# Two vector-matrix products of a diffusion step, moved from TensorE strips to VectorE sums

## The chip, the cores and the metric

The kernel runs on one core of a Trainium2 chip. The metric is device time in microseconds (us) of one execution. The kernel before takes 1458.52 us (median of 3 runs, 1456.28 to 1462.25).

## The reference: what is computed

One layer of a hybrid backbone works on 128 context tokens and 512 latent tokens of width 2048, in float32. Cut to what matters here:

```python
silu_c, silu_ctx = silu(c), silu(c_ctx)[None]
mod_ctx = silu_ctx @ w_mod[i] + b_mod[i]            # (1, 6144): shift, scale, gate
mod_lat = silu_c @ w_mod[i] + b_mod[i]
h = _rms_norm(x, norm_w) * (1.0 + scale[:, None]) + shift[:, None]
proj = h @ w_in                                     # 2048 -> 7216: u_f, z_f, q, k, v, z_d, a, b
y_f = _fourier_mix(u_f, grid) * silu(z_f)           # 4 groups of 128 columns
o_fw, s_fw = _chunk_gated_delta(q, k, v, ...)       # 12 heads of 128, forward and backward
y_d = _rms_norm(o, gnorm_w) * silu(z_d)
y = concatenate([y_f, y_d]) @ w_out
x + gate[:, None] * y                               # then a final RMS norm
```

Two pieces of it are products of a vector with a matrix, each for two vectors (latent and context): the gate third of `mod`, which is `silu(c) @ w_mod[:, 4096:6144]` and the same with `c_ctx`, and the shift's share of the Fourier inputs, `shift @ w_in[:, 0:512]`. The second exists because the kernel multiplies `x * scale` without the shift, and adds the shift's product as a bias of each column afterwards.

## The kernel before, in words

**The stream.** The input projection runs on TensorE as 53 column tiles of 128 columns ("u" Fourier inputs, "f" their gates, "k", "v", "q", "z" of the heads). Float32 is split into a high and a low part, so a tile takes three products for each of 16 blocks of 128 rows, for each of two halves of 320 tokens: 96 products, all at line 1354 (`stream`). The weights are cast to the high part by ScalarE (line 1330) and subtracted to the low part by GpSimd (line 1338).

**The heads.** A head's q, k and v go through convolution, the blocks of its triangular matrix, their inversion (`solve`, lines 872 to 945), `decay` (lines 950 to 1000), `prep` (1005 to 1050) and the scan (1058 to 1143). These are small products on TensorE (lines 929, 940, 973, 994, 1012, 1025, 1040, 1047, 1072, 1079, 1091, 1099, 1111) with VectorE, ScalarE and GpSimd work and small transfers through memory between them. `solve` writes its blocks to memory and reads them back as tiles DD and DP by eight transfers (lines 912 and 915); VectorE transposes DD (line 918) and TensorE multiplies with it (line 929). The k and q tiles of head h may only be evacuated when head h-2 has been scanned.

**What sets the order.** Each step is a Python generator. While the program is written, a planner (`Estimate`, lines 55 to 210) keeps an estimated clock for every engine. It writes stream products, and between any two steps of six products it lets every generator go on whose inputs are due by that estimate; smaller ranks go first. So the order on every engine is fixed when the program is built, and each engine runs its own queue in order. `yield "V", t` means "go on when VectorE is free and estimated time t has come", `"P"` the same for TensorE, `"S"` for the queue SP that issues transfers.

**The two vector products before.** `rows256` (line 1264) works on 256 columns at a time. It loads four blocks of 128 rows by one transfer of 512 KB into the tile gw (line 1269), and multiplies: four products, each with one column strip of 32 of TensorE's array, whose stationary operand is the two vectors padded with zeros to 32 columns (line 1273). VectorE adds the four results to ga (lines 1276 and 1278). After four such loads one product with `sel_mod` (a matrix of zeros and ones) adds the four strips (lines 1260 and 1291). `shift_u` calls it twice, `res_gates` eight times, so line 1273 holds 40 groups of four products. They have the largest rank, 10, of all steps. The tile gw is one buffer. A product of two float32 operands stands as two instructions in the profile.

**Names.** csh and cz are the two vectors (shift, silu of c), of 16 x 32 columns, of which the first two of each 32 hold them. gates_d is the gates' row in memory, which the output stage reads back. L1622 is the output product.

## Time and profile before

| | us |
|---|---|
| median of 3 runs | 1458.52 |
| lowest, highest | 1456.28, 1462.25 |
| the profiled execution's own time | 1462.74 |
| its span, first to last instruction | 1460.9 |
| TensorE busy in the span | 1400.6 |
| VectorE busy | 695.1 |
| ScalarE busy | 670.8 |
| GpSimd busy | 627.6 |

The span is the time from the first to the last instruction on the core; 1.8 us of the execution lie outside it. PE is TensorE, DVE VectorE, ACT ScalarE, POOL GpSimd, SP the queue that issues transfers. A product's row gives its start and how long it stays in the array; since products are pipelined, the step from one start to the next is what a product costs in a row of them.

### The profile page before, as it was taken

The page shows a single profiled execution, that of the slowest core. Times are in us where ns is not written, and L with a number is a line of the kernel's source. Part 1 is how long each engine was busy: PE and PEld are TensorE (multiplying, and loading weights), DVE is VectorE, ACT ScalarE, POOL GpSimd, SP SyncE. Part 2 cuts the span into 40 slices and gives each one's busy share as a digit, 9 for nine tenths or more (in the row PEclk, how much of TensorE's full clock was granted, in tenths as well). Part 3 has the DMA queues.
Part 4 walks back from the last instruction along what each step waited for, and adds up shares of the span by engine and source line. Part 5 has one row for each costly group of instructions (what it writes and reads, how often), then busy time and mean ns, then how long its engine had stood idle before and what let it go on. Part 6 is the DMA issues. An engine that isn't in the chain of part 4 may idle for free.

```text
span 1460.9 us, 31546 instructions
## 1 busy us (share of the span) xinstructions
PE 1400.6 (96%) x12548; PEld 1272.2 (87%) x12548; DVE 695.1 (48%) x1476; ACT 670.8 (46%) x1808; POOL 627.6 (43%) x649
## 2 busy tenths in 40 slices
PE   6999989999999999999999999999999998999996
PEld 4799869878999889889999999899999996888885
DVE  5441115664346644746474646457463745322025
ACT  5332226634456445354555555455555454323134
POOL 2233213443334534344464544545364442337375
PEclk9999989999999999999999999999999999999998
DMA  9988973553454533433233333333242435494103
GB/s 304 271 264 267 309 202 105 151 147 102 140 146 123 141 124 95 144 106 90 83 91 87 86 107 83 106 87 106 72 112 62 137 111 178 148 323 163 44 1 144
DMA packets 268880, 203.21 MB, mean 139 GB/s; under 512 B 54649, under 2 KB 238918, under 8 KB 268606
## 3 DMA queue, kind: packets, MB, share of 16 engines
q1 hardware_dynamic: 146110, 129.36, 28.9%
q10 hardware_dynamic: 122624, 71.84, 17.1%
q8 instruction: 99, 1.62, 0.5%
q14 instruction: 47, 0.39, 0.1%
HBM read 177.16 MB, written 23.99 MB: 138 GB/s over the span
## 4 chain that ended last, share of the span: by engine, by line
PE 75%; DVE 9%; DMA 6%; ACT 2%; SPq 2%; issue 2%; POOL 1%; DVEq 0%; ACTq 0%; POOLq 0%
PE mbank L1354 40%; PE bank L1622 8%; PE mbank L1622 7%; PE bank L430 2%; DVE tmp L898 2%; PE bank L1091 1%; DMA DD<-xd 1%; PE bank L1111 1%; PE bank L1099 1%; PE bank L1072 1%; DVE tmp L885 1%; PE bank L1079 1%; PE bank L1273 1%; PE bank L587 1%; SPq L875 1%
## 5 line engine op out<-in xcount | busy, mean ns | idle before, releaser
L1338 POOL TENSOR_TENSOR wlo<-raw,whi 128x512 fp32r<-128x512 f32 x232 | 327.0, 1413 | 550.4 <-ACT whi L1330 463.0
L1354 PE MATMUL mbank<-h_hi,whi 128*128 128x320 f32 (+1 forms) x1696 | 556.0, 328 | 0.0
L1354 PE MATMUL mbank<-h_lo,whi 128*128 128x320 f32 (+1 forms) x1696 | 528.0, 311 | 0.0
L1354 PE MATMUL mbank<-h_hi,wlo 128*128 128x320 f32 (+1 forms) x1696 | 527.9, 311 | 0.0
L1354 PEld LDWEIGHTS mbank<-h_hi,whi 128*128 128x128 f32 x1696 | 321.9, 190 | 24.7 <-issue 20.3
L1354 PEld LDWEIGHTS mbank<-h_lo,whi 128*128 128x128 f32 x1696 | 322.3, 190 | 0.1
L1354 PEld LDWEIGHTS mbank<-h_hi,wlo 128*128 128x128 f32 x1696 | 321.9, 190 | 0.0
L1330 ACT CAST whi<-raw 128x512 fp32r<-128x512 f32 x232 | 142.2, 619 | 226.1 <-PE mbank L1354 155.3
L283 POOL TENSOR_TENSOR wlo<-raw,whi 128x512 fp32r<-128x512 f32 (+1 forms) x44 | 55.2, 1264 | 87.0 <-ACT whi L282 72.8
L1622 PE MATMUL mbank<-wlo,y_hi 128*128 128x512 f32 x160 | 63.7, 398 | 2.6 <-POOL wlo L283 2.0
L1622 PE MATMUL mbank<-whi,y_lo 128*128 128x512 f32 x160 | 64.1, 401 | 2.1 <-DVE y_lo L1509 2.0
L1622 PE MATMUL mbank<-whi,y_hi 128*128 128x512 f32 x160 | 64.1, 401 | 1.3 <-ACT y_hi L1507 1.3
L1094 ACT ACTIVATE vn<-bank,s 128x128 f32<-128x128 f32 x120 | 37.4, 364 | 57.1 <-PE bank L1091 56.7
L1622 PE MATMUL bank<-whi,y_hi 128*128 128x512 f32 x160 | 63.2, 395 | 0.0
L1622 PE MATMUL bank<-wlo,y_hi 128*128 128x512 f32 x160 | 63.1, 395 | 0.0
L1622 PE MATMUL bank<-whi,y_lo 128*128 128x512 f32 x160 | 63.1, 395 | 0.0
L1106 DVE SCALAR_TENSOR_TENSOR S<-S,egl,bank 128x128 f32<-128x128 f32 x72 | 21.8, 344 | 77.7 <-PE bank L1099 77.6
L282 ACT CAST whi<-raw 128x512 fp32r<-128x512 f32 (+1 forms) x44 | 24.6, 578 | 57.0 <-PE bank L1622 18.6
L885 DVE TENSOR_TENSOR tmp<-NP,XB 40x4 f32<-40x4 f32 (+6 forms) x84 | 31.1, 371 | 33.3 <-DMA NP<-pd 26.6
L1084 POOL TENSOR_SCALAR kd<-k,edl 128x128 f32<-128x128 f32 x96 | 45.4, 487 | 0.3
L977 ACT ACTIVATE E<-gb,ngg 128x128 f32<-128x128 f32 x120 | 40.2, 397 | 11.6 <-DVE AT L980 9.3
L829 POOL TENSOR_TENSOR nk<-sk,cst 128x5 f32<-128x5 f32 x12 | 14.1, 1179 | 63.2 <-DVE sk L826 56.3
(336 smaller groups left out, 2452.7 us busy)
## 6 DMA issues: line engine op xcount, KB each, us to landing
raw<-in_w_in ACTq DMA_DIRECT2D x106, 512.0 KB
wm<-in_w_mod SPq DMA_DIRECT2D x64, 512.0 KB
gw<-in_w_mod SPq DMA_DIRECT2D x32, 512.0 KB
raw<-in_w_out ACTq DMA_DIRECT2D x48, 256.0 KB
gb<-gd SPq DMA_DIRECT2D x12, 640.0 KB
yd<-zs SPq DMA_DIRECT2D x16, 320.0 KB
yt<-yd SPq DMA_DIRECT2D x16, 320.0 KB
out<-res SPq DMA_DIRECT2D x10, 512.0 KB
```

The lines of the kernel that those rows point to most:

```text
L282: ACT.copy(whi, raw_part)
L283: sub.tensor_tensor(wlo, raw_part, whi, ALU.subtract)
L430: PE.matmul(acc_a[i][:, 0:384], lhsT=w, rhs=h[kt][:, 256:NT], start=kt + n == 0, stop=last)
L885: DVE.tensor_tensor(tv, NPd[:, :, i, 0:i].unsqueeze(2).broadcast_to(s4), Xd[:, :, 0:i, 0:i].rearrange("p h j c -> p h c j"), ALU.mult)
L898: DVE.tensor_tensor(tv, A.unsqueeze(2).broadcast_to(s4), B.rearrange("p j c -> p c j").unsqueeze(1).broadcast_to(s4), ALU.mult)
L977: ACT.activation(E[:, 1 - d], gb[:, d, P * t:P * (t + 1)], AF.Exp, bias=ngg4[:, d, h, t:t + 1])
L1084: POOL.tensor_scalar(kd[:, d], k[:, tt[d], :], edl4[:, d, h, tt[d]:tt[d] + 1], 1.0, ALU.mult, ALU.mult)
L1094: ACT.mul(vn[:, d], pv[:, P * d:P * (d + 1)], s["s3"][:, d, tt[d]:tt[d] + 1])
L1330: ACT.copy(his[c], raws[c // 2][:, 4 * (c % 2):4 * (c % 2) + 4])
L1338: POOL.tensor_tensor(lo, raws[c // 2][:, 4 * (c % 2):4 * (c % 2) + 4], his[c], ALU.subtract)
L1354: PE.matmul(pm[:, 0:b - a], lhsT=w, rhs=h[k][:, a:b], start=k + m == 0, stop=k == NK - 1 and m == 2)
L1622: PE.matmul(acc[t], lhsT=a[kk][:, sl], rhs=w, start=kk == order[0] and j == 0, stop=kk == order[-1] and j == 2)
```

## The change

`rows256` no longer multiplies on TensorE. It loads two blocks of 128 rows (256 KB) at a time into the first half of the tile gw, and VectorE multiplies each block with one column of csh or cz, a value for each partition, and adds it to a sum for each of the two vectors in the other half of the tile. So the 2048 rows are summed to 128 partitions. The partitions are then summed by a product with ones: in `shift_u` four products of one column instead of two of two columns, in `res_gates` four strips of 32 columns, each for 128 of the columns of one vector, instead of one product with `sel_mod`. The bias b_mod is loaded, and the gates stored, by four transfers each instead of one.

Two planner rules are changed: a transfer now keeps the issuing queue for 0.4 us of the estimate instead of 0.06, and `solve` goes on to its transpose of DD only when 1.5 us have passed since the estimated landing. The Fourier gate tile f2, which stood between f1 and k2, stands after z10, in front of f3.

```diff
         if by == "DMA":
-            self.free[engine] = t + 0.06
+            self.free[engine] = t + 0.4
...
-        yield "V"
+        yield "V", est.written(DD) + 1.5
         f2, N = "p d t c -> p (d t c)", s["N"]
         DVE.transpose(DD[:, 2:4].rearrange(f2), DD[:, 0:2].rearrange(f2))
...
+    def rows256(src, by):
+        x = g.tile([P, 4, 256], F32, tag="gw", name="gw", bufs=1)
+        gw, acc = x[:, 0:2], x[:, 2:4]
+        for j in range(NK // 2):
+            SP.dma_start(out=gw, in_=src[:, 2 * j:2 * j + 2])
+            yield "V", est.last + 1.0
+            for q in range(2):
+                for m in range(2):
+                    one = by[:, 2 * j + q, m:m + 1]
+                    if j + q:
+                        DVE.scalar_tensor_tensor(acc[:, m], gw[:, q], one, acc[:, m], ALU.mult, ALU.add)
+                    else:
+                        DVE.tensor_scalar(acc[:, m], gw[:, q], one, None, ALU.mult)
+        yield
+        return x
...
-            ga = yield from rows256(win_v[:, :, 256 * i:256 * i + 256], csh)
+            x = yield from rows256(win_v[:, :, 256 * i:256 * i + 256], csh)
             pg = bank()
             for q in range(2):
-                PE.matmul(pg[:, 2 * q:2 * q + 2], lhsT=ga[:, P * q:P * (q + 1)], rhs=K("sel_mod"), start=True, stop=True)
+                for m in range(2):
+                    PE.matmul(pg[:, 2 * q + m:2 * q + m + 1], lhsT=x[:, 2 + m, P * q:P * (q + 1)], rhs=K("ones")[:, 0:1],
+                              start=True, stop=True)
...
-        for j in range(4):
-            gw = g.tile([P, 4, 256], F32, tag="gw", name="gw", bufs=1)
-            SP.dma_start(out=gw, in_=src[:, 4 * j:4 * j + 4])
-            yield "P", est.last + 3.0
-            pg = bank()
-            for q in range(4):
-                PE.matmul(pg[32 * q:32 * q + 32, 0:256], lhsT=lhs[:, 4 * j + q, :], rhs=gw[:, q, :], start=True, stop=True,
-                          tile_position=(0, 32 * q))
...
+            for b in range(4):
+                SP.dma_start(out=bt[32 * b:32 * b + 32], in_=b_mod[0, n0 + P * (b % 2):n0 + P * (b % 2) + P].partition_broadcast(32))
             yield "P", est.last + 1.0
             pg = bank()
-            PE.matmul(pg[0:2, 0:256], lhsT=K("sel_mod"), rhs=ga, start=True, stop=True)
-            DVE.tensor_tensor(bt, bt, pg[0:2, 0:256], ALU.add)
+            for b in range(4):
+                PE.matmul(pg[32 * b:32 * b + 32, 0:P], lhsT=K("ones")[:, 0:32], rhs=x[:, 2 + b // 2, P * (b % 2):P * (b % 2) + P],
+                          start=True, stop=True, tile_position=(0, 32 * b))
+            DVE.tensor_tensor(bt, bt, pg[:, 0:P], ALU.add)
...
-    names = "u0 u1 u2 u3 k1 q1 v1 z0 z1 f0 f1 f2".split()
-    fill = {2: "", 11: "z10 f3 z11"}
+    names = "u0 u1 u2 u3 k1 q1 v1 z0 z1 f0 f1".split()
+    fill = {2: "", 11: "z10 f2 f3 z11"}
```

Since the planner writes the order, rows move on every engine. Lines behind 1310 stand six lines lower in the changed file (L1354 is L1360 there, L1622 is L1628).

The first place is TensorE's queue in the scan of head 0. L1099 and L1111 end a scan step, L1072 and L1079 begin the next with the state S, L1091 uses r, which VectorE makes at line 1075. Before:

```order
L1099 MATMUL bank<-vn,kd 128x128 x2
L1111 MATMUL bank<-vn,AT 128x128 x2
L1354 MATMUL mbank<-h_hi,whi 128x320
L1354 MATMUL mbank<-h_lo,whi 128x320
L1354 MATMUL mbank<-h_hi,wlo 128x320
...
L1072 MATMUL bank<-S,KT 128x128 x2
L1079 MATMUL bank<-S,QT 128x128 x2
L1273 MATMUL bank<-gw,cz 32x256 x4
L1091 MATMUL bank<-r,KK 128x128 x2
```

And with the change:

```order
L1099 MATMUL bank<-vn,kd 128x128 x2
L1111 MATMUL bank<-vn,AT 128x128 x2
L1072 MATMUL bank<-S,KT 128x128 x2
L1079 MATMUL bank<-S,QT 128x128 x2
L1360 MATMUL mbank<-h_hi,whi 128x320
L1360 MATMUL mbank<-h_lo,whi 128x320
L1360 MATMUL mbank<-h_hi,wlo 128x320
...
L1091 MATMUL bank<-r,KK 128x128 x2
```

The four strips of line 1273 are gone, and stream products stand between line 1079 and line 1091 where they stood.

The second place is VectorE's queue at the start of the scan of head 1 (the row of L1125 is its first). Before:

```order
L1125 TENSOR_TENSOR o<-o,bank 128x128
L1075 SCALAR_TENSOR_TENSOR r<-bank,neg_eg,v 128x128 x2
L795 SCALAR_TENSOR_TENSOR zs<-zs,pj_1297 128x128
L795 SCALAR_TENSOR_TENSOR zs<-zs,pj_1297 128x512
L1276 TENSOR_TENSOR ga<-ga,bank 128x256
L1106 SCALAR_TENSOR_TENSOR S<-S,egl,bank 128x128 x2
L1121 TENSOR_TENSOR o<-o,bank 128x128 x2
```

With the change:

```order
L1125 TENSOR_TENSOR o<-o,bank 128x128
L1075 SCALAR_TENSOR_TENSOR r<-bank,neg_eg,v 128x128 x2
L1264 SCALAR_TENSOR_TENSOR gw<-gw,cz 128x256 x4
L826 TENSOR_SCALAR sk<-sk 128x5
...
L1106 SCALAR_TENSOR_TENSOR S<-S,egl,bank 128x128 x2
L1121 TENSOR_TENSOR o<-o,bank 128x128 x2
L1264 SCALAR_TENSOR_TENSOR gw<-gw,cz 128x256 x4
L1075 SCALAR_TENSOR_TENSOR r<-bank,neg_eg,v 128x128 x2
```

Batches of four multiply-adds of the loaded rows stand ahead of S (line 1106) and of r (line 1075), on which the next products of the scan wait. There are 80 such batches in all, the last ahead of the stream's 4260th product of 5088; the last use of line 1273 stood behind its 2442nd.

The third place is the end of the stream on TensorE, where head 11 is scanned. Before, the last scan products stand in a row, behind the stream's last product and ahead of the first output product (L1622):

```order
L1354 MATMUL mbank<-h_hi,wlo 128x322
L1099 MATMUL bank<-vn,kd 128x128 x2
L1111 MATMUL bank<-vn,AT 128x128 x2
L1072 MATMUL bank<-S,KT 128x128 x2
L1079 MATMUL bank<-S,QT 128x128 x2
L1091 MATMUL bank<-r,KK 128x128 x2
L1111 MATMUL bank<-vn,AT 128x128 x2
L1214 MATMUL bank<-dft,uT 128x256
```

With the change:

```order
L1099 MATMUL bank<-vn,kd 128x128 x2
L1111 MATMUL bank<-vn,AT 128x128 x2
L1360 MATMUL mbank<-h_hi,whi 128x322
...
L1072 MATMUL bank<-S,KT 128x128 x2
L1079 MATMUL bank<-S,QT 128x128 x2
L1360 MATMUL mbank<-h_hi,whi 128x322
...
L1091 MATMUL bank<-r,KK 128x128 x2
L1214 MATMUL bank<-dft,fx 128x256 x2
L1360 MATMUL mbank<-h_hi,whi 128x322
...
L1111 MATMUL bank<-vn,AT 128x128 x2
```

Six stream products stand between each of the last steps of the scan now, and 96 more behind its last product.

More of the change, by code (lines that the diff above doesn't have):

```diff
@@ L1263, in shift_u @@
         done.add("ubias")
-    def rows256(src, lhs):
-        ga = g.tile([P, 256], F32, tag="ga", name="ga", bufs=1)
-        for j in range(4):
-            gw = g.tile([P, 4, 256], F32, tag="gw", name="gw", bufs=1)
-            SP.dma_start(out=gw, in_=src[:, 4 * j:4 * j + 4])
-            yield "P", est.last + 3.0
-            pg = bank()
-            for q in range(4):
-                PE.matmul(pg[32 * q:32 * q + 32, 0:256], lhsT=lhs[:, 4 * j + q, :], rhs=gw[:, q, :], start=True, stop=True,
-                          tile_position=(0, 32 * q))
-            if j:
-                DVE.tensor_tensor(ga, ga, pg[:, 0:256], ALU.add)
-            else:
-                DVE.tensor_copy(ga, pg[:, 0:256])
-        yield
-        return ga
     def res_gates():
@@ L1284, in res_gates @@
         for i in range(8):
-            ns = slice(2 * DM + 256 * i, 2 * DM + 256 * i + 256)
-            ga = yield from rows256(wmv[:, :, ns], cz)
-            bt = g.tile([P, 4, 256], F32, tag="gw", name="gbt", bufs=1)[0:2, 0]
-            SP.dma_start(out=bt, in_=b_mod[0, ns].partition_broadcast(2))
+            n0 = 2 * DM + 256 * i
+            x = yield from rows256(wmv[:, :, n0:n0 + 256], cz)
+            bt = x[:, 0, 0:P]
+            for b in range(4):
+                SP.dma_start(out=bt[32 * b:32 * b + 32], in_=b_mod[0, n0 + P * (b % 2):n0 + P * (b % 2) + P].partition_broadcast(32))
             yield "P", est.last + 1.0
             pg = bank()
-            PE.matmul(pg[0:2, 0:256], lhsT=K("sel_mod"), rhs=ga, start=True, stop=True)
-            DVE.tensor_tensor(bt, bt, pg[0:2, 0:256], ALU.add)
+            for b in range(4):
+                PE.matmul(pg[32 * b:32 * b + 32, 0:P], lhsT=K("ones")[:, 0:32], rhs=x[:, 2 + b // 2, P * (b % 2):P * (b % 2) + P],
+                          start=True, stop=True, tile_position=(0, 32 * b))
+            DVE.tensor_tensor(bt, bt, pg[:, 0:P], ALU.add)
             yield "S"
-            SP.dma_start(out=gates_d[:, 256 * i:256 * i + 256], in_=bt)
+            for b in range(4):
+                SP.dma_start(out=gates_d[b // 2:b // 2 + 1, 256 * i + P * (b % 2):256 * i + P * (b % 2) + P], in_=bt[32 * b:32 * b + 1])
             yield
```

## The prediction

> **What bounds the kernel now.** I read the page first, then TensorE's time line around one of the removed groups, then busy time by stretch, then who waited for whom.
>
> ```profile
> span 1460.9 us, 31546 instructions
> PE 1400.6 (96%) x12548; PEld 1272.2 (87%) x12548; DVE 695.1 (48%) x1476; ACT 670.8 (46%) x1808; POOL 627.6 (43%) x649
> ...
> PE 75%; DVE 9%; DMA 6%; ACT 2%; SPq 2%; issue 2%; POOL 1%; DVEq 0%; ACTq 0%; POOLq 0%
> ...
> L1354 PE MATMUL mbank<-h_hi,wlo 128*128 128x320 f32 (+1 forms) x1696 | 527.9, 311 | 0.0
> ```
>
> TensorE is busy for 96% of the span, and the stream (line 1354) never stood idle for its inputs (last column 0.0). The chain that ended last runs over TensorE for 75% and over others for a quarter: TensorE is the bound, but the heads' small steps are close behind it. By stretch (window, length, then busy us of each engine, the granted clock behind POOL):
>
> ```profile
> 205.00:663.00 458.00, 440.40 (x4396) 400.55 (x4397) 241.18 (x529) 228.05 (x639) 184.81 (x205) 0.97 0.44 127
> 663.00:1075.00 412.00, 408.49 (x4171) 398.42 (x4170) 239.68 (x500) 219.57 (x633) 203.19 (x211) 1.00 0.33 90
> 205.00:1075.00 870.00, 848.90 (x8564) 798.97 (x8565) 480.86 (x1028) 447.63 (x1272) 388.00 (x415) 0.99 0.39 109
> ```
>
> The 40 groups of line 1273 run in the first of these; TensorE is idle there for 17.6 us of 458, and for 3.5 of the next 412. A product taken off TensorE here should therefore come off the span, unless a wait takes its place.
>
> **What the change removes from TensorE.** One group of four strips, alone in the stream (start, length, then what it is):
>
> ```profile
> 293.03 0.31 PE L1354 MATMUL mbank<-h_lo,whi 128*128 128x320 f32 x1
> 293.18 0.31 PE L1354 MATMUL mbank<-h_hi,wlo 128*128 128x320 f32 x1
> 293.42 0.64 PE L1273 MATMUL bank<-gw,cz 128*32 128x256 f32 x8
> 293.99 0.41 PE L1354 MATMUL mbank<-h_hi,whi 128*128 128x320 f32 x1
> ```
>
> Stream products start 0.15 us apart. Around the group two starts are 0.81 apart, so the group costs 0.66 us. Forty of them: 26.4 us. The busy time of the two groups of rows of this line agrees (20.4 and 5.9 us):
>
> ```profile
> L1273 PE MATMUL bank<-gw,cz 128*32 128x256 f32 x256 | 20.4, 390 | 0.0
> L1273 PE MATMUL bank<-gw,csh 128*32 128x256 f32 x64 | 5.9, 448 | 0.9 <-DMA gw<-in_w_in 0.9
> ```
>
> The sums over strips, in the same view of time (start to next start):
>
> ```profile
> 331.95 0.59 PE L1291 MATMUL bank<-ga,cst 128*2 128x256 f32 x2
> 332.47 0.41 PE L1354 MATMUL mbank<-h_hi,whi 128*128 128x322 f32 x1
> ...
> 298.33 0.48 PE L994 MATMUL bank<-jq,cst 128*32 128x160 f32 x8
> 298.74 0.41 PE L1354 MATMUL mbank<-h_hi,whi 128*128 128x320 f32 x1
> ...
> 240.04 0.50 PE L1260 MATMUL bank<-cst,ga 128*128 128x2 f32 x4
> 240.41 0.39 PE L1354 MATMUL mbank<-h_hi,whi 128*128 128x320 f32 x1
> ```
>
> Line 1291 costs 0.52 us, eight times 4.2. In its place stand four strips with ones; line 994 is the same product with 160 columns instead of 128 and costs 0.41, so at most 3.3 for eight. Line 1260 is two products for 0.37; four products of one column instead cost at most twice that, so the two calls go from 0.7 to 1.5. TensorE's net work: -26.4 - 4.2 + 3.3 - 0.7 + 1.5 = **-26.5 us**. The tile f2 costs the same where it stands now.
>
> **What else moves.** TensorE's waits from 205 to 1215 us, from the waits by engine (who waited for what, total us, times, longest):
>
> ```profile
> PE bank L929 <- DVE DD L918: 8.9, 9, 3.3
> PE bank L1260 <- DVE ga L1276: 1.0, 1, 1.0
> PE bank L1273 <- DMA gw<-in_w_in: 0.9, 2, 0.6
> PE bank L1111 <- ACT vn L1094: 0.8, 1, 0.8
> PE bank L1091 <- DVE r L1075: 0.6, 1, 0.6
> PE bank L1291 <- ACT KK L844: 0.3, 1, 0.3
> ```
>
> The waits of lines 1273, 1260 and 1291 (2.2 us) go with their products, or come back once as VectorE's. Those of lines 1111 and 1091 (1.4 us) are the two last steps of head 11's scan, which had no stream product between them. Now f2 lies there: **-1.4**. The f2 tile's 96 products (96 x 0.15 = 14 us) are missing between f1 and k2, but nothing there waits: k2's evacuation needs head 0's scan, whose last product stands 54 stream products ahead of it.
>
> L929 waits for the transpose of DD, and that for the eight transfers of DD and DP, which SP issues one after the other:
>
> ```profile
> 288.13 0.31 SPq L912 DMA_DIRECT2D DD<-xd  x1
> 288.50 0.45 SPq L915 DMA_DIRECT2D DP<-xd  x1
> ```
>
> One issue takes 0.31 to 0.45 us; the planner had reckoned 0.06, so it believed DD there some 8 x 0.35 = 3 us too early. With 0.4 and the margin of 1.5 us the transpose and its product are written later, and the wait can be filled with stream products. Between 0 and all of it: 0 to -8.9; one long wait there also cost clock:
>
> ```profile
> 606.00:609.70 3.70, 1.24 (x83) 1.20 (x84) 0.51 (x1) 0.37 (x3) 0.52 (x1) 1.00 0.45 123
> 609.70:613.10 3.40, 3.40 (x13) 2.23 (x11) 0.41 (x1) 0.70 (x3) 0.00 (x0) 0.50 0.34 104
> ```
>
> After 2.5 us of idleness the clock is granted at 0.50 for 3.4 us, which is another 1.7. I take half the 8.9, **-4.5**, as the other half may be a wait of which the queue's issue is not the cause.
>
> **What it adds on VectorE.** 300 multiply-adds and 20 multiplications of 128x256; the 40 additions and copies of ga go. No multiply-add of this size from SBUF is in the trace. The nearest is line 979, the same size with both inputs in SBUF (minimum, median, maximum ns, then the mean); with it, GpSimd's subtraction of the stream's low parts, and the additions that go:
>
> ```profile
> L979 DVE TENSOR_TENSOR KK<-KK,E x60: 380/412/1521, 265.3 to 1160.2; 128x256 f32<-128x256 f32 x60
> L979 DVE TENSOR_TENSOR KK<-KK,E 128x256 f32<-128x256 f32 x60 | 33.4, 557 | 1.5 <-ACT E L977 1.4
> L1338 POOL TENSOR_TENSOR wlo<-raw,whi x232: 1262/1289/2266, 96.0 to 1278.0; 128x512 fp32r<-128x512 f32 x116
> L1276 DVE TENSOR_TENSOR ga<-ga,bank 128x256 f32<-128x256 f32 x30 | 12.4, 414 | 24.3 <-PE bank L1273 24.1
> ```
>
> Between 412 and 557 ns each; I take the mean, since GpSimd works through the same stretch as beside line 979: 320 x 0.557 = 178 us, less 40 x 0.414 = 17 for the ga operations, so 161. VectorE was busy for 481 of the 870 us over which the batches now lie: 55% becomes 74%. The work itself is covered. If it were not, the uncovered part would come on top of the span one for one.
>
> The Trainium skill ("SBUF — State Buffer", section "Who interferes with whom") says that a VectorE instruction with two SBUF inputs contends with a GpSimd instruction that reads SBUF, and that whichever is second is fully blocked. Line 979's maximum, 1.1 us above its median, is as long as most of one subtraction, so the trace agrees; by that rule all 300 multiply-adds are such instructions. It is the reason for the second case below, whose sum stands on the rows above.
>
> What does not hide is lateness: VectorE's queue is in order, and r and S of the scan stand behind batches. A batch is late by its load and by GpSimd. The load: line 1273 waited 0.9 us in two waits, 0.45 each, with a margin of 3.0 us; with 1.0 I allow 0 to 0.45 per batch, up to 36 us for 80. GpSimd: 4 x (557-412) = 0.58 per batch, up to 46. How much of VectorE's lateness reaches TensorE shows in what it suffers from transfers now:
>
> ```profile
> DVE tmp L885 <- DMA NP<-pd: 26.6, 7, 7.3
> DVE DD L918 <- DMA DD<-xd: 9.2, 5, 3.3
> DVE tmp L885 <- DMA gbt<-in_b_mod: 4.5, 1, 4.5
> DVE DD L918 <- DMA DP<-xd: 3.0, 2, 1.6
> ```
>
> That is 43.3 us, of which TensorE felt 8.9, a fifth. A fifth of 82 is 17: between 0 and +17, and I take the middle, **+8**.
>
> SP issues 88 transfers more (40 loads of gw, 24 of b_mod, 24 stores of the gates); at 0.4 us that is 35 us over 870, on a queue that mostly waits. The packets stay 1 KB. The gates are ready at the 4260th stream product instead of the 2466th, still ahead of the Fourier steps that ask for them at the end of the stream.
>
> **The sum**: -26.5 - 2.2 - 1.4 - 4.5 + 8 = -26.6. The span goes from 1460.9 to 1434.3, the profiled execution from 1462.74 to 1436.1; the median of the runs shown lies 4.2 under that execution, so 1458.5 - 26.6 = **1432 us**. With the ends of the bounds: -26.5 - 2.2 - 1.4 - 8.9 - 1.7 = -41 gives 1418, and -26.5 - 2.2 + 17 = -12 gives 1447.
>
> **The rivals.**
>
> *Lateness eats half* (15%). All of the 82 us is real, and TensorE feels a quarter of it instead of the tenth I took, since r and S stand right behind batches: +21 in place of +8, so -26.5 - 2.2 - 1.4 - 4.5 + 21 = -14, some 1445. For it: the batch ahead of r in head 1's scan. Against it: the planner's own estimate of such an operation (0.54 us) is already the mean of line 979.
>
> *The saved time turns into idleness* (8%). If the heads, not TensorE, set the pace, TensorE waits where it worked: about 1457. For it speaks the quarter of the chain that is not TensorE's; against it the 0.0 of line 1354 and 17.6 us of idleness in 458.
>
> *Slower: SP's head of line* (10%). The tile gw is one buffer, so the next load stands at the head of SP until the batch has been added, and behind it stand the transfers of the heads (NP, DD, gb, S).
>
> ```profile
> SPq L1269 <- PE bank L1273: 95.5, 25, 9.5
> SPq L1269 <- DMA gw<-in_w_mod: 40.1, 13, 4.4
> SPq L1269 <- DMA gw<-in_w_in: 13.4, 4, 3.7
> ```
>
> SP stood 149 us for 40 loads, 3.7 each; now there are 80, and they wait for VectorE, which is fuller. If one such hold delays each of the ten heads that run beside the batches, and TensorE, in order, waits it out each time with the clock's 1.7 behind it, that is 10 x (3.7 + 1.7) = 54 us: 1458.5 - 30 + 54 = 1482. It decides from 3 us a head. Against it: the nine waits for DD made 1 us a head, with half the loads.
>
> *More than forecast* (7%): all of the DD wait goes and lateness is hidden: 1418.
>
> **How the numbers follow.** My forecast has 60%, its own range 1418 to 1447. I let the range end at 1456, which takes in half of the lateness case and nearly the idle one, and leaves out the slow case and a little on both ends: 1418 to 1456. A measurement of this kernel tells about 0.5% from none, that is 7.3 us. Faster by more: forecast, lateness and more than forecast, less a little, 0.80. Within: the idle case and some of the lateness, 0.10. Slower: 0.10.
>
> **What would show it.** Line 1273 is gone, and the sum of TensorE's busy time falls by about 26 us, to about 1374, with no idle time at line 1360. VectorE is busy for some 850 us; the multiply-adds have a mean between 412 and 557 ns. The wait of line 929 for DD is under 5 us. TensorE's waits for VectorE's r and S and for what follows a batch stay under 17 us. I am wrong if TensorE's busy time falls and the span does not: then the waits by engine name VectorE behind line 1264, or SP behind line 1258, as what TensorE waited for.

## The result, and the profile after

The changed kernel takes 1451.39 us (median of 6 runs, 1447.81 to 1454.38) against 1458.57 for the kernel before beside it (6 runs, 1455.55 to 1462.25). The ratio is 0.9946, with an interval of 0.9928 to 0.9963: it is faster, by about 0.5%, and inside the range, but 7 us of gain came out where 26.6 had been forecast.

Below, a gain in us is always (1 - ratio) x 1458.5, so that kernels timed on different occasions can stand side by side. The change gains 7.9 by that reckoning (5.4 to 10.5).

The page of the changed kernel first (span; busy time by engine; the multiply-adds of `res_gates`, with busy us, mean ns, and what the idle time ahead of them waited for):

```profile
span 1452.6 us, 31431 instructions
...
PE 1378.0 (95%) x12284; PEld 1270.2 (87%) x12284; DVE 849.8 (59%) x1756; ACT 671.2 (46%) x1808; POOL 631.4 (43%) x649
...
L1264 DVE SCALAR_TENSOR_TENSOR gw<-gw,cz 128x256 f32<-128x256 f32 x240 | 133.8, 615 | 22.9 <-DMA gw<-in_w_mod 22.9
```

TensorE's busy time fell by 22.6 us (26.5 had been forecast) and VectorE's rose by 155 (161 forecast). But the span fell by only 8.3. Where the work taken away went is seen when the span is cut at the first output product (line 1622 before, 1628 after). Before, in two stretches (window, length, busy us by engine, granted clock behind POOL), from the first stream product to there, and from there to the end:

```profile
109.10:1210.20 1101.10, 1073.54 (x10795) 1007.18 (x10793) 569.17 (x1267) 542.12 (x1529) 476.52 (x511) 0.99 0.43 124
1210.20:1460.90 250.70, 234.44 (x1019) 188.23 (x1017) 75.60 (x108) 82.50 (x161) 121.82 (x97) 0.98 0.42 144
```

After, the same two, and the stretch in which the sums lie:

```profile
108.20:1209.20 1101.00, 1055.83 (x10561) 1009.40 (x10559) 727.19 (x1571) 546.07 (x1542) 480.39 (x511) 0.99 0.44 125
1209.20:1452.60 243.40, 229.58 (x987) 184.19 (x987) 72.46 (x84) 79.06 (x147) 121.75 (x97) 0.98 0.42 145
...
205.00:1075.00 870.00, 830.00 (x8482) 801.26 (x8481) 638.87 (x1323) 454.30 (x1287) 398.08 (x416) 0.98 0.39 111
```

The first stretch is as long as it was, 1101 us. TensorE works 17.7 us less in it and stands idle 17.6 us more (45.2 instead of 27.6): the saved work turned into idleness, one for one. The 7.3 us that can be seen came at the end, where fewer small products stand among the output products (987 rows instead of 1019); part of the Fourier work, which stood there, now stands in the first stretch, so the work taken off TensorE in that stretch is larger than 17.7 by what moved in. Between 205 and 1075 us TensorE is idle for 40.0 us, where the prediction read 21.1 before.

Whom TensorE waited for, the rows that matter here (total us, times, longest):

```profile
PE bank L775 <- DVE KT L761: 7.9, 3, 4.8
PE bank L1278 <- DVE gw L1264: 6.5, 1, 6.5
PE bank L929 <- DVE DD L918: 5.9, 4, 2.0
PE bank L1072 <- DVE S L1106: 5.6, 4, 1.6
...
PE bank L1091 <- DVE KK L1050: 1.4, 1, 1.4
...
PE mbank L1360 <- POOL wlo L1344: 1.0, 2, 0.5
```

All but the last name VectorE. Before, DD had stood for 8.9 us and S (the state) for 1.1; KT (the convolved keys) and the sums themselves are new. How the multiply-adds ran (minimum, median, maximum ns; then, from the groups by shape, the multiplications that begin each sum, and the other multiply-adds):

```profile
L1264 DVE SCALAR_TENSOR_TENSOR gw<-gw,cz x240: 439/478/1561, 366.6 to 1014.2; 128x256 f32<-128x256 f32 x120
...
L1266 DVE TENSOR_SCALAR gw<-gw,cz 128x256 f32<-128x256 f32 x16 | 8.7, 585 | 0.0
...
L1264 DVE SCALAR_TENSOR_TENSOR gw<-gw,csh 128x256 f32<-128x256 f32 x60 | 31.3, 581 | 8.7 <-DMA gw<-in_w_in 8.7
...
374.47 1.66 DVE L1264 SCALAR_TENSOR_TENSOR gw<-gw,cz 128x256 f32<-128x256 f32 x4
```

The multiply-adds of a batch overlap, so their rows' means (615 and 581 ns) are longer than what each adds to VectorE's busy time: (133.8 + 31.3) / 300 = 0.550 us, against 0.557 taken. For the same reason an ordinary batch, the last line, takes 1.66 us, which is four times 0.412, the lower of the two lengths that the prediction had read from line 979. So 165.1 - 300 x 0.412 = 42 us is time over the ordinary length, and VectorE waited 22.9 + 8.7 = 31.6 us for loads. One place shows what a stretched batch can do (start, length, engine, line; in brackets the idle time ahead and its releaser), and the clock behind it:

```profile
414.06 5.33 POOL L1344 TENSOR_TENSOR wlo<-raw,whi 128x512 fp32r<-128x512 f32 x3
419.36 2.95 POOL L965 TENSOR_TENSOR gb<-gb,cst 128x640 f32<-128x640 f32 x2
...
416.73 5.86 DVE L1264 SCALAR_TENSOR_TENSOR gw<-gw,cz 128x256 f32<-128x256 f32 x4
422.52 0.87 DVE L752 SCALAR_TENSOR_TENSOR KT<-pj,cw,KT 128x641 f32<-128x641 f32 x1
...
425.12 0.83 DVE L761 SCALAR_TENSOR_TENSOR KT<-th,KT 128x641 f32<-128x641 f32 x1 [0.80 <-ACT th L759]
...
426.00 1.11 PE L775 MATMUL bank<-cst,KT 128*128 128x128 f32 x4 [4.78 <-DVE KT L761]
...
426.00:429.40 3.40, 3.40 (x15) 3.40 (x16) 1.79 (x5) 2.41 (x11) 0.00 (x0) 0.50 0.43 76
```

GpSimd works without a pause from 414.06 to 422.31, with three subtractions and two additions. In that time a batch of four multiply-adds takes 5.86 us instead of 1.66. KT stands behind the batch in VectorE's queue, TensorE's next product stands behind KT, and TensorE is idle for 4.78 us and runs the next 3.4 us, the last line, at half clock.

### The profile page after: what moved, and what is told of

It is laid out like the page before. It is cut to its first block, busy times and chain, and to the rows that moved or that the text cites. A ratio compares the mean times of both kernels' runs of the same rounds, so it can differ in the third digit from the quotient of the medians.

```text
span 1452.6 us, 31431 instructions
## 1 busy us (share of the span) xinstructions
PE 1378.0 (95%) x12284; PEld 1270.2 (87%) x12284; DVE 849.8 (59%) x1756; ACT 671.2 (46%) x1808; POOL 631.4 (43%) x649
## 5 line engine op out<-in xcount | busy, mean ns | idle before, releaser
L1360 PE MATMUL mbank<-h_hi,whi 128*128 128x320 f32 (+1 forms) x1696 | 557.8, 329 | 0.0
L1360 PE MATMUL mbank<-h_hi,wlo 128*128 128x320 f32 (+1 forms) x1696 | 529.2, 312 | 1.0 <-POOL wlo L1344 1.0
L1360 PE MATMUL mbank<-h_lo,whi 128*128 128x320 f32 (+1 forms) x1696 | 529.2, 312 | 0.0
L1360 PEld LDWEIGHTS mbank<-h_hi,whi 128*128 128x128 f32 x1696 | 323.8, 191 | 11.4 <-issue 7.9
L1360 PEld LDWEIGHTS mbank<-h_hi,wlo 128*128 128x128 f32 x1696 | 323.2, 191 | 1.6 <-POOL wlo L1344 1.5
L1360 PEld LDWEIGHTS mbank<-h_lo,whi 128*128 128x128 f32 x1696 | 324.0, 191 | 0.1
L1264 DVE SCALAR_TENSOR_TENSOR gw<-gw,cz 128x256 f32<-128x256 f32 x240 | 133.8, 615 | 22.9 <-DMA gw<-in_w_mod 22.9
L1628 PE MATMUL mbank<-wlo,y_hi 128*128 128x512 f32 x160 | 63.9, 400 | 2.6 <-POOL wlo L283 2.0
L1628 PE MATMUL mbank<-whi,y_hi 128*128 128x512 f32 x160 | 64.1, 401 | 1.6 <-ACT y_hi L1513 1.6
L1628 PE MATMUL mbank<-whi,y_lo 128*128 128x512 f32 x160 | 64.0, 400 | 0.5 <-DVE y_lo L1515 0.2
L1628 PE MATMUL bank<-whi,y_lo 128*128 128x512 f32 x160 | 63.1, 395 | 0.0
L1628 PE MATMUL bank<-wlo,y_hi 128*128 128x512 f32 x160 | 63.1, 394 | 0.0
L1628 PE MATMUL bank<-whi,y_hi 128*128 128x512 f32 x160 | 63.0, 393 | 0.0
L1084 POOL TENSOR_SCALAR kd<-k,edl 128x128 f32<-128x128 f32 x96 | 48.4, 517 | 9.4 <-PE bank L1099 9.2
L282 ACT CAST whi<-raw 128x512 fp32r<-128x512 f32 (+1 forms) x44 | 24.6, 578 | 57.6 <-PE bank L1628 18.6
L965 POOL TENSOR_TENSOR gb<-gb,cst 128x640 f32<-128x640 f32 x24 | 38.5, 1622 | 26.9 <-DMA gb<-gd 26.8
L977 ACT ACTIVATE E<-gb,ngg 128x128 f32<-128x128 f32 x120 | 41.3, 397 | 18.2 <-DVE AT L980 12.2
L1106 DVE SCALAR_TENSOR_TENSOR S<-S,egl,bank 128x128 f32<-128x128 f32 x72 | 21.6, 340 | 45.7 <-PE bank L1099 45.7
```

Of the source, the lines that this page charges most:

```text
L282: ACT.copy(whi, raw_part)
L965: POOL.tensor_tensor(gv, gv, masks[d].unsqueeze(1).broadcast_to([P, 5, P]), ALU.add)
L977: ACT.activation(E[:, 1 - d], gb[:, d, P * t:P * (t + 1)], AF.Exp, bias=ngg4[:, d, h, t:t + 1])
L1084: POOL.tensor_scalar(kd[:, d], k[:, tt[d], :], edl4[:, d, h, tt[d]:tt[d] + 1], 1.0, ALU.mult, ALU.mult)
L1106: DVE.scalar_tensor_tensor(Sn[:, d], S[:, d], egl4[:, d, h, tt[d]:tt[d] + 1], pu[:, P * d:P * (d + 1)], ALU.mult, ALU.add)
L1264: DVE.scalar_tensor_tensor(acc[:, m], gw[:, q], one, acc[:, m], ALU.mult, ALU.add)
```

## The experiments

The theory to test is that VectorE's added time ate the gain. Its rivals are that the removed work was never worth 30 us, that the loads (SP's queue and the waits for them) are the cause, and that the planner's rules or the place of f2 are. All kernels were timed against the kernel before on the same chip, in turns.

### The parts of the change by themselves

Kernel e1 is the kernel before with the two planner rules and the late f2, and the strips kept on TensorE; e2 is the change with the old rules and the early f2; e3 is the change with f2 back between f1 and k2.

```diff
 e1: the kernel before, with
-            self.free[engine] = t + 0.06
+            self.free[engine] = t + 0.4
-        yield "V"
+        yield "V", est.written(DD) + 1.5
-    names = "u0 u1 u2 u3 k1 q1 v1 z0 z1 f0 f1 f2".split()
-    fill = {2: "", 11: "z10 f3 z11"}
+    names = "u0 u1 u2 u3 k1 q1 v1 z0 z1 f0 f1".split()
+    fill = {2: "", 11: "z10 f2 f3 z11"}
 e2: the change, with these four edits undone
 e3: the change, with the last two undone
```

> The kernel before with the planner's two new rules (0.4 us of the issuing queue for a transfer, 1.5 us behind the landing of DD) and with f2 late; the two vector products stay TensorE strips. Prediction's terms: the DD wait of 8.9 us falls to half, the last scan's 1.4 us goes, so 1458.5 - 6 = 1452. If that is right, nearly the whole gain of the change (7 us) comes from here and the moved products give nothing. Rival: the rules give nothing or cost, and the moved products bring the 7 us: 1457 to 1462.

> The changed kernel with the planner's old rules and f2 between f1 and k2; only the two vector products are VectorE sums. If VectorE's lateness eats the 26.5 us of TensorE's work, whatever the rules: 1455 to 1462. If the old rules, which believe loads there too early, make it worse still: over 1462. If the new rules or the late f2 are what cost the saving: 1432 to 1440.

> The changed kernel with f2 back between f1 and k2. The trace of the change shows the output products beginning 1.0 us earlier than before and the part behind them 7.4 us shorter, because the Fourier products of that part are done inside the stream. If the late f2 is what brings that, 1456 to 1460 here; if the early end of the heads brings it, 1451 as with the change.

| kernel | median us | ratio, interval | gain us |
|---|---|---|---|
| e1, rules and f2 alone | 1459.25 | 0.998 (0.9957 to 1.0002) | 2.9 |
| e2, sums alone | 1471.76 | 1.0067 (1.0044 to 1.0091) | -9.8 |
| e3, change with f2 early | 1457.75 | 0.9963 (0.9942 to 0.9984) | 5.4 |

Whom TensorE waited for in e1:

```profile
PE bank L929 <- DVE DD L918: 9.9, 5, 3.4
```

and in e2:

```profile
PE bank L929 <- DVE DD L918: 22.6, 10, 5.6
PE bank L1072 <- DVE S L1106: 8.2, 3, 3.4
```

The rules alone did not shorten the wait for DD (9.9 us, 8.9 before), so nothing here shows that this wait came from the issue time that the estimate had left out, as I had half believed. But the sums without the rules make the kernel slower, with a DD wait of 22.6 us. The two parts are worth 2.9 and -9.8, together -6.9, and the change gains 7.9: some 15 us come only from having both. It is the rules that keep the sums from hurting more: e3 differs from e2 in them alone, and gains 5.4 where e2 loses 9.8. The place of f2 cannot be told from nothing: the intervals of e3 and of the change overlap. In e3 the stretch to the first output product is shorter and the one behind it longer:

```profile
107.00:1192.00 1085.00, 1042.84 (x10465) 998.52 (x10464) 710.21 (x1516) 540.17 (x1517) 489.06 (x509) 0.98 0.45 126
1192.00:1453.60 261.60, 242.73 (x1084) 195.37 (x1082) 81.97 (x139) 86.48 (x171) 122.23 (x99) 0.99 0.41 138
```

Beside the change's 1101.0 and 243.4 these are 16.0 us less and 18.2 more. Where a kernel passes to its output stage is not a gain by itself; only the sum of both stretches counts.

### Is it the wait for the loads?

Kernel e4 lets a batch start 3.0 us behind its estimated landing instead of 1.0. Kernel e6 loads blocks of 128 rows into two buffers in turn, each load issued a block ahead.

```diff
 e4
-            yield "V", est.last + 1.0
+            yield "V", est.last + 3.0
 e6
-        for j in range(NK // 2):
-            SP.dma_start(out=gw, in_=src[:, 2 * j:2 * j + 2])
+        SP.dma_start(out=x[:, 0], in_=src[:, 0])
+        for j in range(NK):
             yield "V", est.last + 1.0
+            if j + 1 < NK:
+                SP.dma_start(out=x[:, (j + 1) % 2], in_=src[:, j + 1])
```

> The changed kernel with one number changed: a batch of multiply-adds is written 3.0 us behind the estimated landing of its load instead of 1.0. Load theory (VectorE, in order, stands 31.6 us for these loads, and TensorE waits behind it): that idle time goes below 5 us, TensorE's waits fall by 10 us or more, 1438 to 1443. Lock theory (multiply-adds that meet GpSimd's subtraction last 1.5 us instead of 0.48, and what is queued behind them is late): the loads do not matter, 1449 to 1453, with the multiply-adds' mean still near 0.6 us.

> The changed kernel with blocks of 128 rows (128 KB) in two buffers in turn: a load is issued when the batch before it is written, into the buffer that the batch before that has read, so it never stands on SP for VectorE; batches have two multiply-adds instead of four, 160 loads instead of 80. Queue theory (SP held for VectorE delays DD's loads): the time from the issue of xd to DD's first load goes from 2.5 to 7.9 us back to about 2.5, 1436 to 1445. Load and lock theories, which this leaves (margin and multiply-adds the same): 1448 to 1455; 80 more issues of 0.4 us on SP may cost a little.

e4 took 1489.69 us, ratio 1.0193 (1.0151 to 1.0236): 28 us slower than before. e6 took 1453.50, ratio 0.994 (0.9919 to 0.9961), the same as the change. VectorE's waits for loads did fall in e4:

```profile
DVE gw L1264 <- DMA gw<-in_w_mod: 6.4, 4, 3.8
...
DVE gw L1264 <- DMA gw<-in_w_in: 1.4, 2, 0.8
```

from 31.6 to 7.8 us, but the last multiply-add then starts at 1238.7 us instead of 1014.2. The gates come too late for the Fourier steps, which ask for them, and these run behind the stream:

```profile
L1264 DVE SCALAR_TENSOR_TENSOR gw<-gw,cz x240: 437/475/1559, 413.9 to 1238.7; 128x256 f32<-128x256 f32 x120
...
1191.10:1486.00 294.90, 253.24 (x1100) 201.68 (x1098) 99.68 (x191) 91.79 (x181) 122.57 (x98) 0.93 0.40 136
```

That last stretch is 51.5 us longer than the change's 243.4, which is more than the whole loss. TensorE's wait for DD grew as well, to 23.7 us. So e4 is no clean test of the load wait: its order changed, and the late gates show a second limit that the prediction named only as slack. e6 is no clean test either, since its order changed with it (the stretch up to the output became 1073.8 us, the rest 267.9). That is why the next runs keep the order.

### The same order, with one cost taken away

In e9 a multiply-add works on 16 of its 256 columns, and the planner is told the full length, so that the order on every engine is that of the change; in all but the first batch of a sum the other columns are left out. In e10 only the first of the eight loads of a sum goes to gw; the other seven bring half their bytes to a tile that nobody reads, and the planner is told of gw, so the order of all engines but for SP's target stands; all eight batches of a sum then work on its first two blocks. e11 does both. e5 is e10 with the order planned anew.

```diff
 e9
-                    one = by[:, 2 * j + q, m:m + 1]
+                    one, w = by[:, 2 * j + q, m:m + 1], 16 if j else 256
-                        DVE.scalar_tensor_tensor(acc[:, m], gw[:, q], one, acc[:, m], ALU.mult, ALU.add)
+                        DVE.scalar_tensor_tensor(acc[:, m, 0:w], gw[:, q, 0:w], one, acc[:, m, 0:w], ALU.mult, ALU.add)
 e10 (e5 without the first line)
+            est.alias = gw
-            SP.dma_start(out=gw, in_=src[:, 2 * j:2 * j + 2])
+            if j == 0:
+                SP.dma_start(out=gw, in_=src[:, 0:2])
+            else:
+                SP.dma_start(out=g.tile([P, 256], F32, tag="ga", name="gx", bufs=1), in_=src[:, 2 * j])
```

> The changed kernel, but only the first load of each eight goes to the rows that VectorE reads; the other seven load one block of 128 rows (half the bytes) to a place that nothing reads, and the sums are formed from the first load again and again (the gates and shift rows are therefore not the reference's). So VectorE never waits for such a load, and SP never stands before one until a batch is done; the number and length of the multiply-adds stay. Load and queue theory (VectorE's 31.6 us of waits for gw, and DD's loads held behind gw's on SP): TensorE's idle time in the stream falls from 45 to about 28 us and its half-clock time with it, 1430 to 1437. Lock theory (only the 1.5 us multiply-adds beside GpSimd matter): 1447 to 1452.

> The changed kernel with every multiply-add behind the first load of each eight cut to 16 of its 256 columns, and the planner told the full length: the order is the same row for row on every engine, loads and all. Only VectorE's time for the sums is left out (so the gates and shift rows are not the reference's). If VectorE's length is what delays TensorE: the batches of 1.7 to 5.9 us shrink to about 1, TensorE's idle time in the stream falls by 10 us or more, 1437 to 1443. If the loads are: 1446 to 1452, with VectorE's waits for gw as long as before (31.6 us) or longer.

> As the experiment with loads laid aside, but with the planner told of the old loads: the order of every engine is that of the changed kernel row for row. All loads but the first of each eight go, half as large, to a place that nothing reads (the sums are wrong by that). If the loads hold VectorE and SP: VectorE's 31.6 us of waits for gw go, xd to DD's first load is 2.5 us, TensorE's idle time falls by 10 us or more, 1437 to 1443; if that experiment's gain was its other order, 1446 to 1452.

> Both at once, still in the same order: multiply-adds of 16 columns and loads that nobody waits for. What is left is TensorE without the strips. If VectorE's lateness by loads and lengths is the whole of what went missing: TensorE idle for about 25 us in the stream, 1430 to 1436, which is the prediction's 1432 with its +8 taken out (1424) to in. If the planner's order itself costs (steps written later than before): 1440 or more.

| kernel | median us | ratio, interval | gain us |
|---|---|---|---|
| the change | 1451.39 | 0.9946 (0.9928 to 0.9963) | 7.9 |
| e5, loads aside, new order | 1439.85 | 0.9852 (0.9825 to 0.9879) | 21.6 |
| e10, loads aside | 1445.00 | 0.9874 (0.9844 to 0.9904) | 18.4 |
| e9, short multiply-adds | 1435.44 | 0.9811 (0.9786 to 0.9836) | 27.6 |
| e11, both | 1434.16 | 0.9804 (0.9777 to 0.983) | 28.6 |

This decides two of the questions. First, the removed work is worth about what the prediction said: with VectorE's part made small, the kernel gains 27.6 to 28.6 us, and the terms of the prediction without lateness and without the DD term (-26.5 - 2.2 - 1.4) are -30.1, inside both intervals. (TensorE's wait for DD is down to 2.2 us in e9, from 8.9; that is in these gains too.) Second, nearly 20 us of it (27.6 - 7.9) are lost through VectorE's time. Taking the loads away returns 10 by itself, but adds nothing that can be told once VectorE is short. That fits the view that the end of a batch is what hurts, to which its wait for the load and its length both contribute. Nor can e5 be told from e10: their intervals overlap.

The two stretches of e9, then its multiply-adds (16 columns wide; busy us, mean ns, and the wait for loads), then an ordinary batch, then the one that stood at 416.73 us in the change:

```profile
108.20:1190.60 1082.40, 1048.78 (x10562) 1004.88 (x10559) 642.75 (x1571) 545.84 (x1542) 473.61 (x511) 0.99 0.45 127
1190.60:1433.00 242.40, 228.00 (x987) 183.04 (x987) 73.68 (x84) 79.35 (x147) 122.62 (x97) 0.99 0.43 145
...
L1266 DVE SCALAR_TENSOR_TENSOR gw<-gw,cz 128x16 f32<-128x16 f32 x224 | 62.2, 337 | 18.4 <-DMA gw<-in_w_mod 18.2
L1266 DVE SCALAR_TENSOR_TENSOR gw<-gw,csh 128x16 f32<-128x16 f32 x56 | 15.5, 338 | 5.2 <-DMA gw<-in_w_in 5.2
L1266 DVE SCALAR_TENSOR_TENSOR gw<-gw,cz x240: 186/229/1503, 363.2 to 992.4; 128x16 f32<-128x16 f32 x112, 128x256 f32<-128x256 f32 x8
...
371.07 0.67 DVE L1266 SCALAR_TENSOR_TENSOR gw<-gw,cz 128x16 f32<-128x16 f32 x4
...
414.00 5.04 DVE L1266 SCALAR_TENSOR_TENSOR gw<-gw,cz 128x16 f32<-128x16 f32 x4
...
422.46 0.90 PE L777 MATMUL bank<-cst,KT 128*128 128x128 f32 x3 [4.64 <-DVE KT L763]
```

The same instructions in the same order: the first stretch is 18.6 us shorter, of which 11.6 are idleness (33.6 instead of 45.2) and 7.0 are TensorE's busy time for the same products (1048.8 us instead of 1055.8; the mean granted clock of the execution is 0.989 instead of 0.983). The second stretch is the same to 1.0. And at 414 us four multiply-adds of 16 columns still take 5.04 us, where an ordinary batch takes 0.67, and TensorE still waits 4.64. This part of the loss e9 leaves.

What e9 takes away is, above all, the ordinary length: 1.66 us a batch become 0.67, for 70 of the 80 batches, some 69 us. Of the lateness it leaves most: the waits for loads are 18.2 + 5.2 = 23.4 us instead of 31.6, and the time over the ordinary length is 62.2 + 15.5 - 70 x 0.67 = 31 us for the short multiply-adds, where all of the change's were 42 over. So the 20 us are not the price of the lateness alone.

### Is it GpSimd?

In e8 the sums are kept in a bank of PSUM, the memory in which TensorE's products land, so that a multiply-add has one input in SBUF, where the loaded tiles lie, instead of two. This takes one of the five banks of the small products, so e7, the change with four banks, is the control. e12 is e8 with each load issued a batch ahead, into the half of gw that is free, and a margin of 2.0 us.

```diff
 e7 and e8
-    ps_g = ctx.enter_context(tc.tile_pool(name="ps_g", bufs=5, space=PSUM))
+    ps_g = ctx.enter_context(tc.tile_pool(name="ps_g", bufs=4, space=PSUM))
 e8
+    ps_a = ctx.enter_context(tc.tile_pool(name="ps_a", bufs=1, space=PSUM))
-        gw, acc = x[:, 0:2], x[:, 2:4]
+        gw, acc = x[:, 0:2], ps_a.tile([P, 2, 256], F32, tag="a", name="acc", bufs=1)
...
+        yield "A", est.last
+        ACT.copy(x[:, 2:4], acc)
```

> The changed kernel with four accumulation banks for the small products instead of five: the control for the next kernel, which needs the bank. All theories: the planner's order changes, 1448 to 1462.

> The kernel with four banks, and the two sums of the multiply-adds kept in the fifth, in PSUM, so that a multiply-add has one input in SBUF instead of two; ScalarE copies them to SBUF at the end of eight loads. Lock theory: no multiply-add lasts over 0.9 us (43 of 320 did), their mean goes from 609 to under 480 ns, and the time lies 8 us or more under the control's. Load and queue theory: the long ones may go, but TensorE's waits stay and the time is within 4 us of the control's.

> Four banks, the sums in PSUM (one SBUF input to a multiply-add), and the load of the next two blocks issued, into the other half of gw, when the batch before it is written, so that it never waits on SP; a batch is written 2.0 us behind its load's estimated landing. Everything is computed. Load, queue and lock theories together: VectorE's waits for gw under 5 us, no multiply-add over 0.9 us, 1436 to 1446, the first kernel here that beats the changed one. If the fourth bank's loss (15 us) cannot be had back by both: 1447 to 1455.

e7 took 1475.36 us, ratio 1.0098 (1.0069 to 1.0127); e8 1453.00, ratio 0.9941 (0.9918 to 0.9964); e12 1454.29, ratio 0.9937 (0.9911 to 0.9964). The multiply-adds of e7:

```profile
L1264 DVE SCALAR_TENSOR_TENSOR gw<-gw,cz x240: 438/477/1570, 362.9 to 1023.8; 128x256 f32<-128x256 f32 x120
```

and of e8, with the multiplications that begin a sum:

```profile
L1266 DVE SCALAR_TENSOR_TENSOR acc<-gw,cz,acc x240: 445/490/491, 372.1 to 1026.6; 128x256 f32<-128x256 f32 x120
...
L1268 DVE TENSOR_SCALAR acc<-gw,cz x16: 470/484/490, 371.0 to 972.8; 128x256 f32<-128x256 f32 x16
...
400.41 2.06 DVE L1266 SCALAR_TENSOR_TENSOR acc<-gw,cz,acc 128x256 f32<-128x256 f32 x4
```

With the sums in PSUM none of the 320 instructions is stretched, or held: the longest takes 491 ns, in the same stretch and beside the same subtractions, where it took 1570. That is shown. An ordinary batch takes longer, though: 2.06 us (last line) instead of 1.66. The step is worth 22 us against the control (1475.36 to 1453.00), but that figure is not GpSimd's part alone, since the planner reckons an operation on PSUM shorter and wrote another order. The bank it takes costs as much (e7 loses 14.3 us where the change gains 7.9, more than had been expected), so e8 ends where the change ends. e12 cannot be told from e8; since its margin and its order differ too, it does not test the loads.

### Is it the length of one hold, or the planner's reckoning?

Kernel e13 lets other work of VectorE stand between the multiply-adds of a batch; as run, a step ends after each of the first three, which is one more than its expectation says. e14 tells the planner that each takes 0.9 us instead of 0.54. e15 does both, with the same three ends of a step.

```diff
 e13
+                    if q + m < 2:
+                        yield "V"
 e14
+            if two and "gw" in outs[0].tensor.name and many == 256:
+                return 0.9
```

> The change, but the planner may place other work of VectorE between the multiply-adds of a batch: a step ends after the first and after the third of the four, so that r and S of the scan stand behind at most two of them. All multiply-adds keep their size, their number and their inputs. If the length of one uninterrupted hold of VectorE (1.7 us as a rule, up to 5.9) is what reached TensorE, the ratio falls from 0.9946 towards the 0.9811 of the run with short multiply-adds, to 0.985 to 0.99. If it is VectorE's occupancy as a whole (176 us of batches), it stays at 0.993 to 0.997; if the finer steps delay the gates until the Fourier work has to run behind the stream, it rises to 1.0 or above.

> The change, but the planner reckons 0.9 us for each multiply-add instead of 0.54, which is above the measured mean, so that it leaves room behind a batch for what GpSimd takes. If the planner's too short length is what made r and S late, the ratio falls to 0.985 to 0.99. If the order it writes leaves no other place for the work, it stays at 0.993 to 0.997.

> Both: steps of two multiply-adds and 0.9 us for each. If the two causes add, 0.98 to 0.985; if they are the same, no lower than the better of the two alone; if the sums then end too late for the Fourier work, above 1.0.

e13 took 1510.11 us, ratio 1.0322 (1.0294 to 1.0349); e14 1454.25, 0.9935 (0.9913 to 0.9957); e15 1540.72, 1.0543 (1.0504 to 1.0583). In e13 the last multiply-add starts at 1258.7 us, instead of 1014.2, and the loss lies in the last stretch as in e4, only larger (TensorE's two largest waits, for the sums of `res_gates` and in the Fourier steps; the end of the multiply-adds; and the stretch from the first output product on):

```profile
PE bank L1297 <- DVE gw L1264: 35.1, 1, 35.1
PE bank L1214 <- ACT uT L1187: 15.8, 2, 9.2
...
L1264 DVE SCALAR_TENSOR_TENSOR gw<-gw,cz x240: 435/479/1578, 418.9 to 1258.7; 128x256 f32<-128x256 f32 x120
...
1180.00:1506.10 326.10, 254.82 (x1108) 202.47 (x1106) 103.25 (x204) 91.21 (x179) 120.95 (x97) 0.89 0.37 126
```

So e13 says nothing on the length of a hold; a split that keeps the gates in time was not tried. e15 is the same, and worse: TensorE waits 70.2 us for the sums of `res_gates`. In e14, with 0.9 us, the planner brings the first stretch down, and pays at the end.

```profile
107.90:1200.40 1092.50, 1054.37 (x10536) 1010.08 (x10534) 704.68 (x1562) 541.33 (x1536) 474.22 (x511) 0.98 0.45 126
1200.40:1453.70 253.30, 235.14 (x1013) 188.54 (x1013) 74.04 (x93) 81.66 (x153) 122.46 (x98) 0.98 0.41 141
```

8.5 us less, then 9.9 more. A longer reckoned length does not by itself bring the gain back: with room left behind the batches, the stretch from the output's start holds more (1013 products' rows instead of 987, and 18.2 us of idleness instead of 13.8). No run of a complete kernel beats the change; e6, e8, e12 and e14 (0.9935 to 0.9941) cannot be told from it.

## Why the prediction was right and wrong

**Right: the work taken off TensorE.** The sum of -26.5 for the products stands. TensorE's busy time fell from 1400.6 to 1378.0 where 1374 was forecast, and to 1369.3 in e9, where it waits less and the clock is better. e9 and e11, with VectorE's part short, gain 27.6 and 28.6 of the 30.1 us that the terms without lateness and DD make. The stream has stayed without waits, but for 1.0 us. That the cost of a group was read from start to start in the stream (0.66 us), and not from its busy time, is what made this term good.

**Right: how busy VectorE gets.** It is busy 849.8 us where some 850 was forecast, with 0.550 us for each multiply-add where 0.557 was taken. The means of the rows, 615 and 581 ns, do lie above the 412 to 557 that the prediction named as a sign, because the instructions of a batch overlap; the lines that it read, of line 979, do not show that.

**Wrong: "+8" as all that VectorE costs.** This is the step that failed. The +8 was made of a bound of 82 us for what VectorE could be late, times a fifth, halved; the ordinary length of the batches stood at nothing ("the work itself is covered", at 74% busy). The lateness itself came out within its bound: 31.6 us of load waits (36 allowed) and 42 us over the ordinary length (46 allowed), 73 in all. But TensorE lost about 20 us through VectorE (27.6 of e9 less the change's 7.9, and e9 leaves some). And e9 gets these back while it leaves at least 54 of the 73 us of lateness (23.4 + 31); what it takes away is mostly the ordinary length. So two things were wrong: the price, 8 instead of about 20, and the view that only lateness has one. VectorE was 73% busy between 205 and 1075 us, as forecast, and still not free.

Why the fifth was too small can only be argued. It had been read from VectorE's waits for transfers in the heads' solve (lines 885 and 918), and other steps stand behind a batch than behind those: KT, the sums' own products, S and DD are the names in TensorE's waits after (7.9 + 6.5 + 5.6 + 5.9 us). The first three alone make 20.0, above the 17 that the prediction had set as the limit. Nor was the new waiting all added to the old. Of the waits from which the share was read, the largest fell from 26.6 us to

```profile
DVE tmp L885 <- DMA NP<-pd: 5.2, 4, 2.9
```

**Wrong: "-4.5" for DD.** e1 makes the same edit alone and the wait is 9.9 us (8.9 before). In the change it is 5.9, above the 5 that I had named as the limit, so 3.0 us less than before. The rules did something else that I had not reckoned at all: e2 shows that the sums without them lose 9.8 us, so their worth lies in taking up part of what the sums add.

**Not told: -2.2 and -1.4.** These waits are too small for any run to tell by themselves. The first came back as VectorE's, as the prediction allowed: line 1278 waited 6.5 us once, for the sums of `shift_u`.

**The rivals.** "Lateness eats half", given 15%, had nearly the right price: +21 where about 20 was measured. It came to 1445 because it kept the DD term; without that it is about 1449, and 1451.4 was measured. That is in part luck: it charges the lateness alone, and e9 leaves most of that and loses little. "The saved time turns into idleness" has the right look (17.6 us more idleness up to the output), but its cause, a pace set by the heads, is refuted by e9, which keeps the heads' work and its order and gains 27.6 us. "SP's head of line" was not seen as a loss of its own: SP did stand for longer, 115.9 + 57.8 us in these rows against 149 before,

```profile
SPq L1258 <- DVE gw L1264: 115.9, 39, 14.8
...
SPq L1258 <- DMA gw<-in_w_mod: 57.8, 27, 4.3
```

but in e9 the same two rows still make 92.6 + 54.6 us, nearly the 149 of before, and the loss is gone; e10, which frees the loads from waiting for a batch, halves their bytes and takes VectorE's waits for them away, returns about half. The 54 us of this rival were not seen.

**The rule beside the rows.** The rule of the Trainium skill that the prediction set beside its rows ("SBUF — State Buffer", section "Who interferes with whom") is borne out here. That section says also that a VectorE instruction with at most one SBUF input, outside the modes that use both ports, does not contend: in e8 none of 320 was stretched. I had turned the rule into a mean length. That gave the busy time, but it hides that an ordinary batch takes 1.66 us and a single one 5.86, behind which the convolution stood.

**What stays open.** How the 20 us divide between the batches' ordinary length, GpSimd's hold and the waits for loads is not settled. e9 takes away most of the ordinary length and leaves most of the rest; e10 takes away the waits for loads; e8 takes away the hold and makes the ordinary length greater. They return about 20, 10 and 22 us, so these are not shares that add up, and e8, whose control is e7, changed the order as well. A multiply-add from PSUM in the same order and with all five banks was not tried.

## What to carry to other kernels

Work that is moved to an engine with spare time is not free because it fits: in an in-order queue everything behind it comes later, by its ordinary length as well as by its waits. Read there, one batch at a time and at its longest, who waits for the next instruction. A share of lateness that reaches the bound engine should be taken only from waits ahead of the same consumers. And where a planner fixes the order, test a cost with the order held fixed: the runs that let it change (e4, e6, e13, e14) moved work between the stream and the end, and told little.

## What the runs showed of the hardware that was not expected

That a VectorE instruction's size can hardly matter beside GpSimd's work: four multiply-adds of 16 columns took 5.04 us (an ordinary batch of them 0.67), four of 256 columns 5.86 at the same place. That is one place and not a rule: the batch that took 3.75 us at 242.51 us in the change took 1.78 in e9. And that an instruction with a single SBUF input is stretched too: the 16 multiplications that begin the sums of `res_gates` have a mean of 585 ns in the change, while the same ones written to PSUM take 470 to 490 (e8) and are never longer. The minimum, median and maximum of the former:

```profile
L1266 DVE TENSOR_SCALAR gw<-gw,cz x16: 340/346/1382, 366.1 to 955.3; 128x256 f32<-128x256 f32 x16
```

From SBUF to SBUF it is quicker undisturbed, 346 ns against 484, and can take 1382. The same section of the Trainium skill lists this operation among those that can take the shared port pair in a faster mode; the rows agree with that, though no run here shows the mode itself.
